# A pooling mixer in float32 by fast matrix products: all seven operands of a block kept in HBM between the two input phases

## The chip, the cores and the metric

One core of a Trainium2 chip. The metric is the time of one execution on the device, in microseconds; lower is better. TensorE (PE) multiplies, VectorE (DVE) adds and subtracts, ScalarE (ACT) copies and applies functions, GpSimd (POOL) and SyncE (SP) mostly issue DMAs. Every engine works through its own instructions in order.

## The reference

With `DEPTH = 1` one layer runs: a root-mean-square normalization, a causal pooling mixer, a residual addition and a last normalization, on `x` of 4096 rows by 1024 channels in float32.

```python
def pool_mixer(h, in_w, group_w, group_b, scale, out_w):
    b, s, _ = h.shape
    u, gate = jnp.split(h @ in_w, 2, axis=-1)
    ug = u.reshape(b, s, POOL_GROUPS, POOL_GROUP_DIM)
    pooled = jnp.stack([trailing_mean(ug[:, :, g], w) for g, w in enumerate(POOL_WINDOWS)],
                       axis=2) - ug
    mixed = jnp.einsum('bsgc,gcd->bsgd', pooled, group_w) + group_b
    y = mixed.reshape(b, s, POOL_WIDTH) * scale * jax.nn.silu(gate)
    return y @ out_w

h = h + pool_mixer(rms_norm(h, norm_w[0]), ...)
return rms_norm(h, final_norm_w)
```

## The kernel before, in words

**Products.** A float32 number is split into a high part (ScalarE copies it, which rounds it to fp32r) and a low part (VectorE subtracts the high one); a product takes three passes, high by high, high by low and low by high. Each large product is computed by seven products of half size, P1 to P7, instead of eight, with sums and differences of the quarters as operands (a Winograd form). `w[i]` holds the split weights of product i, `ops` is a ring of four buffers of split operands, two of which one product takes. PSUM has eight banks: P1, P2, P7 and P4 work in banks 0 to 3 ("x", "v"), P6, P5 and P3 in banks 4 to 7 ("y"). P1's result is copied to the y banks, on which P6, P5 and P3 add up; P4 adds to P7's.

**Phases.** The input weight is folded with the group map in the beginning. Then come 28 steps "a" (four blocks of 1024 rows by seven products, order P1, P2, P7, P6, P5, P4, P3) for one half of the output columns, 28 steps "b" for the other half with the same rows, and steps "o" for the output product, eight blocks of 512 rows by seven (order P1, P7, P6, P2, P5, P4, P3). A plain product of a or b has 48 matmuls of 512 columns: 2 halves of the contraction (h), 4 column tiles (ct), 2 tiles of 128 (kk), 3 passes.

**Operands of a and b.** `xs[b]` holds the quarters of a block's normalized rows: "11", "12" (second half of the rows), "21" and "22". In phase a `load_in` fetches them from `x`, `form_in` normalizes them by factors that were computed from `x` a block ahead and that take a way through HBM (`store_rs`, `load_rstd`, both on POOL's queue; `rd`), and forms the operands: "21" becomes 11 - 21 (P7), "2" = 22 - 21 (P6), "11" becomes 11 + "2" (P5), `form_s4` turns "12" into 12 - "2" (P3); P4 takes "22" itself. `split_in` splits an operand and, where `sd[b]` has an entry, stores it to HBM from POOL's queue (512 KB a half). Before the change that is so for P1, P2, P7 and P4. In phase b these four are loaded from `sd` on SP's queue, and "2", "11" and "12" are formed once more. `load` runs three steps ahead of the product, `form` two, `split_step` one.

**Inner P7.** For blocks 1 and 2 of phase b, P7 is itself made of seven products of half its size (`split_seven`, `product_seven`, 84 matmuls of 256 columns; P6's operand is split in its middle). The summed weights lie in three kept buffers (`kept_in`) and in a quarter of `w[P7][0]` that holds another weight in the plain form. `form_seven` prepares them in block 0 of phase b; `load_plain` and `split_plain` bring the plain quarter back in block 2, since block 3 uses the plain P7.

**Output weights.** `make_wo` scales and combines the output weights in blocks 1 and 2 of phase b and stores them to `wod`. In block 3, behind each product i, `load_w(wod, i)` loads that product's output weights (2 x 512 KB) and splits them into `w[i]`, which is free then.

**Output phase.** From block 2 on P7 is an inner product with own weights (`own_into`, prepared by `split_weight(P7, ...)` in steps of block 1), and P2 from block 1 on (`product_inner`, sets "spare" of banks). `add_inner(0, (0, 0))` adds an inner result from a spare bank to the rows; the inner P6 in step P5 writes that bank again. `norm_row` scales a finished row by its factor and sends it to the output. `steady` writes out the order of blocks 2 to 7; in the last block (`final`) the order by hand ends in step P2 (`InOrder.on`), and the scheduler places the rest.

**Order.** The scheduler orders the instructions of an engine by their place in the program and by when it expects their inputs; `tc.issue_after(ins)` puts what it covers behind `ins` on the same engine. `take` gives the buffer that was freed first, of 11 "st" and 8 "vt" (each 512 KB); who takes one that is still read waits.

Of the kernel before, what the change touches and what calls it, by code (L numbers as in the profile page):

```python
# [10 lines left out]
F32 = mybir.dt.float32  # L11
# [9 lines left out]
NB = S // TB  # L21
# [65 lines left out]
def kernel(  # L87
# [115 lines left out]
    def split(dst, src):  # L203
# [17 lines left out]
        for i in range(P1, P7 + 1)  # L221
# [3 lines left out]
            i: [dram.tile([P, 2, H], F32, name=f"sd{b}_{i}_{h}") for h in range(2)]  # L225
            for i in (P1, P2, P7, P4)
        }
# [346 lines left out]
    def load_saved(b, i):  # L574
# [17 lines left out]

    def form_in(q, b, i):

        s = xs[b]
        if i in (P1, P2):
            if q == 0:
                for u in s["11" if i == P1 else "12"]:
                    normalize(b, 0, u)
        elif i == P7:  # L600
            if q == 0:
                for h in range(2):
                    normalize(b, 1, s["21"][h])
                    sub(s["21"][h], s["11"][h], s["21"][h])
        elif i == P6:
            s["2"] = [take(pool=early if (q, b) == (0, 0) else None) for _ in range(2)]
            for h in range(2):
                if q == 0:
                    normalize(b, 1, s["22"][h])
                sub(s["2"][h], s["22"][h], s["21"][h])  # L610
            if not inner_in(q, b, P7):
                for u in s.pop("21"):
                    give(u)
            if q == 0:
                give(rstd.pop(b))
        elif i == P5:
            for h in range(2):
                add(s["11"][h], s["2"][h], s["11"][h])
            if (q, b) != (0, 0) and not inner_in(q, b, P7):
                for u in s.pop("2"):  # L620
                    give(u)

    def inner_in(q, b, i):

        return q == 1 and 0 < b < NB - 1 and i == P7

    def split_in(q, b, i):
        s = xs[b]
        if inner_in(q, b, i):
            return split_seven(s)  # L630
        key = {P1: "11", P2: "12", P6: "2", P7: "21", P5: "11", P4: "22", P3: "12"}[i]
# [62 lines left out]
    def form_seven(stage):  # L694
# [31 lines left out]
        if stage == 3:  # L726
            for u in seven.pop("raw"):
                give(u)

    def load_plain():  # L730
        seven["plain"] = take("p (n k c) -> p n k c", n=2, k=2)
        sync.dma_start(out=seven["plain"][:, 0], in_=t3d[0][:, :, 0:256])

    def split_plain():
        u = seven.pop("plain")
        home = [w[P7][0][:, v, :, 0:256] for v in range(2)]
        copy(home[0], u[:, 0])
        sub(home[1], u[:, 0], home[0].bitcast(F32))
        give(u)

# [626 lines left out]
    def evict_o(b, i, sets):  # L1367
# [4 lines left out]
        if inner and i == P2:  # L1372
            inner["rows"] = [hs[b][0, j][:, 0] for j in range(2)]
        elif inner and i == P5:
            product_inner(P5)
            add_inner(0, (0, 1), (1, 1))
            inner.clear()
            if final:
                for j in range(2):
                    early_half(0, j, 0)  # L1380
        for j in range(2):
# [24 lines left out]
            if last:  # L1406
                factors.append(late_factor(half, j, parts))
                if i == P4 and j == 1 or i == P3 and j == 0:
# [65 lines left out]
    def run(n, between=None, behind=None, seeds=4):  # L1474
# [4 lines left out]
        if kind == "o":  # L1479
            product_out(i, split_up.pop(n), sets, n == len(steps) - 1)  # L1480
            evict_o(b, i, sets)
        else:
            q = 0 if kind == "a" else 1
            if inner_in(q, b, i):
                us, parts = xs[b]["2"], []
                at["split"] += 1

                def next_half():
                    parts.append(split_half(us[len(parts)]))

                product_seven(split_up.pop(n), sets["v"], next_half, next_half)
                if b == NB - 2:
                    give_kept(*places_in)
                split_up[n + 1] = parts
            else:
                product_in(i, split_up.pop(n), sets, i == P1, between, behind)
            if "second" in seven:
                seven.pop("second")()
            evict_in(b, q, i, sets, seeds)
            if "third" in seven:  # L1500
                seven.pop("third")()
            if inner_in(q, b, i):
                form_s4(b)
                for u in xs[b].pop("2"):
                    give(u)
# [3 lines left out]
    def steady(n):  # L1509
# [87 lines left out]
        elif i == P2:  # L1597
# [4 lines left out]
            ready[P4] = next_op("p (s a b) -> p s a b", **whole)  # L1602
            split(ready[P4], s["22"])
            give(s.pop("22"))
            if final:
                norm_row(b - 1, 0, 1)
            InOrder.on = not final
            product_out(P2, ready.pop(P2), sets, False)
            evict_o(b, P2, sets)
        elif i == P5:  # L1610
            sub(s["12"], s["12"], s["11"])
# [6 lines left out]
        elif i == P4:  # L1618
            if not final:
                ahead["12"] = load_y(c, 0, 1)  # L1620
# [233 lines left out]
    def split_reach(kind, b, i):  # L1854
        if kind == "b" and 0 < b < NB - 1 and i == P6:
            return 0
        return 2 if kind == "o" and (b, i) != (0, P1) else 1

    def row_plan(b):
# [16 lines left out]
        (1, P6): lambda: sum_inner(P7),  # L1876
        (1, P5): lambda: split_weight(P7, P7, P6),
        (1, P4): lambda: (split_weight(P7, P5, P3), keep_temps(P7)),
    }
    forming_seven = (P7, P6, P5, P4)  # L1880

    for n in range(2, len(steps)):
# [72 lines left out]
        if kind in ("a", "b"):  # L1955
# [15 lines left out]
            if kind == "b" and b == NB - 1 and i == P3:  # L1971
# [57 lines left out]
```

## Time and profile before

| | |
|---|---|
| median of 3 runs | 906.92 us (906.7 to 907.47) |
| the profiled execution | 907.23 us, of which the span from the first to the last instruction is 905.4 |
| matmuls | 4518 |
| moved by DMA | 180.49 MB, mean 199 GB/s |
| granted TensorE clock | 0.998 of full speed |
| phase a, without what comes ahead of it | about 33 to 323 us |
| phase b | 323 to 613 us |
| phase o | 613 us to the end |

A row of the timeline begins with the start and the length in us, then the engine, the line (L79 is a helper through which all instructions but matmuls go, L807 the plain product, L753 the inner P7 of phase b, L949 the inner products of phase o), the operation, the tile written <- the tiles read, and the count; brackets hold the idle time before it and who ended it. A row of the chain of waits has the start, the length and what. Matmuls overlap, so that one with a length of 0.38 us can follow the one before after 0.22 us; TensorE's pace is found by dividing a stretch by its count.

### The profile page before, as it was taken

Reading aid. Unit: us, or ns where it says so; the run is one execution under the profiler, and the core shown is the slowest. Engines: PE = TensorE matmul, PEld = TensorE weight load, DVE = VectorE, ACT = ScalarE, POOL = GpSimd, SP = SyncE. Lnnn points to the kernel's source line nnn. Section 1 sums busy time; section 2 is a strip of 40 time slices with the busy share of each in tenths; the row PEclk is TensorE's granted clock in tenths of the full one; section 3 lists DMA queues with packets and bytes.
Section 4 is the critical chain, followed back from the end, with each engine's and each line's share of the span. In section 5 each row is a group of like instructions: output and inputs, shape, how many; then the busy total and the mean of one; then the engine's idle time right before and its main releaser. Section 6 shows DMA issues by size and latency. Waiting matters only on the chain.

```text
span 905.4 us, 12216 instructions
## 1 busy us (share of the span) xinstructions
PE 895.8 (99%) x4518; PEld 791.1 (87%) x4518; DVE 757.0 (84%) x925; ACT 517.5 (57%) x853; POOL 118.5 (13%) x208
## 2 busy tenths in 40 slices
PE   9999999999999999999999999999999999999996
PEld 7888888888888888889889888888889899999995
DVE  3899995985995999797599499599798878888797
ACT  7869547547445565346545636654657466565464
POOL 0020100100110000000000000001133333343330
PEclk9999999999999999999999999999999999999999
DMA  9987767577675453333554474638483865945953
GB/s 343 401 305 226 273 239 241 187 274 233 235 267 198 164 199 103 99 112 111 202 199 135 179 279 143 197 117 239 143 236 88 212 180 147 233 153 131 259 181 116
DMA packets 71692, 180.49 MB, mean 199 GB/s; under 512 B 6608, under 2 KB 24656, under 8 KB 71632
## 3 DMA queue, kind: packets, MB, share of 16 engines
q1 hardware_dynamic: 54976, 132.50, 42.6%
q0 software_dynamic: 15936, 46.16, 17.6%
q10 hardware_dynamic: 720, 1.06, 0.3%
q8 instruction: 35, 0.57, 0.3%
q14 instruction: 25, 0.20, 0.1%
HBM read 118.86 MB, written 60.83 MB: 198 GB/s over the span
## 4 chain that ended last, share of the span: by engine, by line
PE 87%; DVE 5%; ACT 3%; DMA 2%; issue 2%; POOL 0%; SPq 0%; DVEq 0%; ACTq 0%; POOLq 0%
PE bank L807 78%; PE bank L949 5%; DVE vt L79 2%; PE bank L753 2%; DVE op L79 2%; DMA st<-yd 1%; PE bank L447 1%; DVE st L79 1%; ACT op L79 1%; DMA early<-in_wut 1%; ACT st L79 1%; ACT w L79 0%; ACT vt L79 0%; DMA st<-wod 0%; DVE w L79 0%
## 5 line engine op out<-in xcount | busy, mean ns | idle before, releaser
L807 PE MATMUL bank<-op,w 128*128 128x512 f32 x2592 | 560.9, 379 | 0.1
L807 PEld LDWEIGHTS bank<-op,w 128*128 128x128 f32 x2592 | 489.4, 189 | 70.3 <-ACT vt L79 0.5
L807 PE MATMUL bank<-w,op 128*128 128x512 f32 (+1 forms) x1044 | 230.5, 377 | 0.0
L807 PEld LDWEIGHTS bank<-w,op 128*128 128x128 f32 x1044 | 192.3, 189 | 25.0
L79 DVE TENSOR_TENSOR op<-st,op 128x1024 fp32r<-128x1024 f32 x116 | 141.0, 1222 | 49.7 <-ACT op L79 49.3
L79 ACT ACTIVATE op<-st 128x1024 fp32r<-128x1024 f32 x116 | 121.4, 1051 | 68.7 <-PE bank L807 27.6
L79 ACT ACTIVATE op<-vt 128x1024 fp32r<-128x1024 f32 x67 | 70.4, 1053 | 59.3 <-DVE vt L79 38.7
L79 ACT ACTIVATE vt<-bank 128x512 f32<-128x512 f32 (+1 forms) x124 | 69.6, 580 | 48.0 <-PE bank L807 44.2
L79 DVE TENSOR_TENSOR op<-vt,op 128x1024 fp32r<-128x1024 f32 x67 | 80.9, 1221 | 17.5 <-ACT op L79 17.4
L79 DVE TENSOR_TENSOR st<-st,st 128x1024 f32<-128x1024 f32 (+1 forms) x55 | 63.9, 1181 | 17.6 <-ACT st L79 16.8
L79 POOL DMA_DIRECT2D vt<-in_x x26 | 23.3, 937 | 390.7 <-DVE vt L79 353.8
L79 ACT ACTIVATE bank<-bank 128x512 f32<-128x512 f32 (+1 forms) x78 | 38.7, 498 | 43.5 <-PE bank L807 32.1
L79 DVE TENSOR_TENSOR vt<-bank,vt 128x512 f32<-128x512 f32 (+1 forms) x94 | 54.2, 603 | 7.1 <-PE bank L949 4.6
L79 ACT ACTIVATE st<-bank 128x512 f32<-128x512 f32 (+1 forms) x58 | 33.0, 587 | 31.2 <-PE bank L807 17.4
L79 ACT ACTIVATE st<-st 128x1024 f32<-128x1024 f32 x33 | 34.8, 1056 | 22.6 <-DVE st L79 19.6
L79 DVE TENSOR_TENSOR st<-bank,st 128x512 f32<-128x512 f32 (+1 forms) x68 | 41.2, 625 | 7.4 <-PE bank L807 4.1
L79 DVE TENSOR_TENSOR st<-st,vt 128x1024 f32<-128x1024 f32 (+1 forms) x36 | 41.6, 1175 | 2.2 <-DMA vt<-rd 2.2
L949 PEld LDWEIGHTS bank<-w,op 128*128 128x128 f32 x312 | 40.4, 191 | 1.7
L949 PE MATMUL bank<-w,op 128*128 128x256 f32 x312 | 41.1, 275 | 0.0
L79 DVE TENSOR_TENSOR w<-st,w 128x1024 fp32r<-128x1024 f32 (+1 forms) x27 | 31.6, 1182 | 9.3 <-ACT w L79 9.2
L79 DVE TENSOR_TENSOR_SCAN vt<-vt,window 128x1040 f32<-128x1040 f32 x16 | 38.0, 2381 | 0.3 <-DMA yd<-vt 0.3
L79 DVE TENSOR_TENSOR vt<-vt 128x1024 f32<-128x1024 f32 (+3 forms) x42 | 37.6, 898 | 0.1
(115 smaller groups left out, 720.7 us busy)
## 6 DMA issues: line engine op xcount, KB each, us to landing
st<-in_xt SPq DMA_DIRECT2D x28, 512.0 KB, 6.2
sd<-st POOLq DMA_DIRECT2D x28, 512.0 KB, 4.4
st<-sd SPq DMA_DIRECT2D x26, 512.0 KB, 4.5
st<-in_x SPq DMA_DIRECT2D x21, 512.0 KB, 6.3
yd<-st SPq DMA_DIRECT2D x19, 512.0 KB, 2.9
vt<-yd SPq DMA_DIRECT2D x17, 512.0 KB, 10.4
out<-vt POOLq DMA_DIRECT2D x17, 512.0 KB, 3.3
st<-wod SPq DMA_DIRECT2D x16, 512.0 KB, 4.3
```

The costliest lines, as they stand in the source:

```text
L79: r = f(*args, **kwargs)
L447: latest[0] = nc.tensor.matmul(ps, a[:, kk, 2 * j + t, :], maps, start=t + m == 0, stop=t == 1 and m == len(pairs) - 1,).ins
L753: latest[0] = nc.tensor.matmul(cell(n, c).rearrange("p (a s) -> p a s", s=2), x1, x2, start=i == P1 and k + m == 0, stop=k == 1 and m == 2 ...
L807: latest[0] = nc.tensor.matmul(ps, a, b, start=start and n == 0, stop=stop and n == 2, skip_group_check=True).ins
L949: latest[0] = nc.tensor.matmul(ps, x1, x2, start=start and k + n == 0, stop=k == 1 and n == 2, skip_group_check=True,).ins
```

## The change

In phase a all seven operands of a block are stored to `sd` (P6's, P5's and P3's are new), and in phase b each of the seven is loaded three steps ahead of its product and its buffers are given back once it is split, so that phase b forms nothing. Block 3 of phase b computes P7 by the inner form too: the kept buffers are held one block longer, and `load_plain` and `split_plain` are gone. In block 3 the output weights of P1 are loaded and split behind P7, those of P2 and P7 behind P6, those of P6 and P5 behind P5, those of P4 and P3 behind their own products as before. In block 1 of phase o the four splits of `split_weight(P7, ...)` all stand in step P4, where two were in step P5. In the last block of phase o the first inner result is added ahead of P2's two evictions, P4's operand is split behind them, and the scaling of one row of the block before (`norm_row(b - 1, 0, 1)`) moves from step P2 to step P4.

```diff
--- before
+++ after
@@ -223,7 +223,7 @@
     sd = [
         {
             i: [dram.tile([P, 2, H], F32, name=f"sd{b}_{i}_{h}") for h in range(2)]
-            for i in (P1, P2, P7, P4)
+            for i in range(P1, P7 + 1)
         }
         for b in range(NB)
     ]
@@ -579,63 +579,59 @@
+    operand = {P1: "11", P2: "12", P7: "21", P6: "2", P5: "11", P4: "22", P3: "12"}
+
     def load_in(q, b, i):
         s = xs[b]
-        if i == P1:
-            s["11"] = load_saved(b, P1) if q else load_x(b, 0, 0)
-        elif i == P2:
-            s["12"] = load_saved(b, P2) if q else load_x(b, 0, 1)
-        elif i == P7:
-            s["21"] = load_saved(b, P7) if q else load_x(b, 1, 0)
-        elif i == P6:
-            s["22"] = load_saved(b, P4) if q else load_x(b, 1, 1)
-
-    def form_in(q, b, i):
+        if q:
+            s[operand[i]] = load_saved(b, i)
+        elif i in (P1, P2, P7, P6):
+            key, *place = {
+                P1: ("11", 0, 0), P2: ("12", 0, 1), P7: ("21", 1, 0), P6: ("22", 1, 1)
+            }[i]
+            s[key] = load_x(b, *place)
+
+    def form_in(b, i):
...
         elif i == P6:
-            s["2"] = [take(pool=early if (q, b) == (0, 0) else None) for _ in range(2)]
+            s["2"] = [take(pool=early if b == 0 else None) for _ in range(2)]
             for h in range(2):
-                if q == 0:
-                    normalize(b, 1, s["22"][h])
+                normalize(b, 1, s["22"][h])
                 sub(s["2"][h], s["22"][h], s["21"][h])
...
     def inner_in(q, b, i):
 
-        return q == 1 and 0 < b < NB - 1 and i == P7
+        return q == 1 and b > 0 and i == P7
 
     def split_in(q, b, i):
...
-        if i == P6 and (q or b):
+        if i == P6 and q == 0 and b:
             form_s4(b)
-        if i not in (P1, P2, P7, P6):
+        if q or i not in (P1, P2, P7, P6):
             for u in s.pop(key):
                 give(u)
         return t
@@ -726,17 +722,6 @@
-    def load_plain():
-        seven["plain"] = take("p (n k c) -> p n k c", n=2, k=2)
-        sync.dma_start(out=seven["plain"][:, 0], in_=t3d[0][:, :, 0:256])
-
-    def split_plain():
-        u = seven.pop("plain")
-        home = [w[P7][0][:, v, :, 0:256] for v in range(2)]
-        copy(home[0], u[:, 0])
-        sub(home[1], u[:, 0], home[0].bitcast(F32))
-        give(u)
@@ -1371,6 +1356,8 @@
         if inner and i == P2:
             inner["rows"] = [hs[b][0, j][:, 0] for j in range(2)]
+            if final:
+                add_inner(0, (0, 0))
...
-        if inner and i == P2:
+        if inner and i == P2 and not final:
             add_inner(0, (0, 0))
@@ -1453,8 +1440,8 @@
     def form(n):
         kind, b, i = step(n)
-        if kind in ("a", "b"):
-            form_in(kind == "b", b, i)
+        if kind == "a":
+            form_in(b, i)
@@ -1489,7 +1476,7 @@
-                if b == NB - 2:
+                if b == NB - 1:
                     give_kept(*places_in)
...
             if inner_in(q, b, i):
-                form_s4(b)
                 for u in xs[b].pop("2"):
                     give(u)
@@ -1600,13 +1586,15 @@
             ready[P4] = next_op("p (s a b) -> p s a b", **whole)
-            split(ready[P4], s["22"])
-            give(s.pop("22"))
-            if final:
-                norm_row(b - 1, 0, 1)
+            if not final:
+                split(ready[P4], s["22"])
+                give(s.pop("22"))
             InOrder.on = not final
             product_out(P2, ready.pop(P2), sets, False)
             evict_o(b, P2, sets)
+            if final:
+                split(ready[P4], s["22"])
+                give(s.pop("22"))
...
         elif i == P4:
-            if not final:
+            if final:
+                norm_row(b - 1, 0, 1)
+            else:
                 ahead["12"] = load_y(c, 0, 1)
@@ -1852,7 +1842,7 @@
     def split_reach(kind, b, i):
-        if kind == "b" and 0 < b < NB - 1 and i == P6:
+        if kind == "b" and b > 0 and i == P6:
             return 0
@@ -1874,8 +1864,7 @@
-        (1, P5): lambda: split_weight(P7, P7, P6),
-        (1, P4): lambda: (split_weight(P7, P5, P3), keep_temps(P7)),
+        (1, P4): lambda: (split_weight(P7, P7, P6, P5, P3), keep_temps(P7)),
@@ -1957,17 +1946,13 @@
             if kind == "b" and b == NB - 1:
-                load_w(wod, i)
+                for p in {P1: (), P2: (), P7: (P1,), P6: (P2, P7), P5: (P6, P5)}.get(i, (i,)):
+                    load_w(wod, p)
             if kind == "b" and b in (1, 2) and i == P7:
                 load_wo(b - 1)
-                if b == NB - 2:
-                    load_plain()
...
-            if kind == "b" and b == NB - 2 and i == P4:
-                with tc.issue_after(latest_copy[0]), tc.issue_after(latest_split[0]):
-                    split_plain()
```

More of the change, by code (lines that the diff above doesn't have):

```diff
@@ L580, in load_saved @@
         return us
+    operand = {P1: "11", P2: "12", P7: "21", P6: "2", P5: "11", P4: "22", P3: "12"}
     def load_in(q, b, i):
         s = xs[b]
-        if i == P1:
-            s["11"] = load_saved(b, P1) if q else load_x(b, 0, 0)
-        elif i == P2:
-            s["12"] = load_saved(b, P2) if q else load_x(b, 0, 1)
-        elif i == P7:
-            s["21"] = load_saved(b, P7) if q else load_x(b, 1, 0)
-        elif i == P6:
-            s["22"] = load_saved(b, P4) if q else load_x(b, 1, 1)
-    def form_in(q, b, i):
+        if q:
[6 more added lines that the diff above has]
+    def form_in(b, i):
         s = xs[b]
         if i in (P1, P2):
-            if q == 0:
-                for u in s["11" if i == P1 else "12"]:
-                    normalize(b, 0, u)
+            for u in s["11" if i == P1 else "12"]:
+                normalize(b, 0, u)
         elif i == P7:
[L601 to L604, printed above, removed]
+            for h in range(2):
+                normalize(b, 1, s["21"][h])
+                sub(s["21"][h], s["11"][h], s["21"][h])
         elif i == P6:
-            s["2"] = [take(pool=early if (q, b) == (0, 0) else None) for _ in range(2)]
+            s["2"] = [take(pool=early if b == 0 else None) for _ in range(2)]
             for h in range(2):
-                if q == 0:
-                    normalize(b, 1, s["22"][h])
+                normalize(b, 1, s["22"][h])
                 sub(s["2"][h], s["22"][h], s["21"][h])
-            if not inner_in(q, b, P7):
-                for u in s.pop("21"):
-                    give(u)
-            if q == 0:
-                give(rstd.pop(b))
+            for u in s.pop("21"):
+                give(u)
+            give(rstd.pop(b))
         elif i == P5:
@@ L618, in form_in @@
                 add(s["11"][h], s["2"][h], s["11"][h])
-            if (q, b) != (0, 0) and not inner_in(q, b, P7):
+            if b:
                 for u in s.pop("2"):
@@ L630, in split_in @@
             return split_seven(s)
-        key = {P1: "11", P2: "12", P6: "2", P7: "21", P5: "11", P4: "22", P3: "12"}[i]
+        key = operand[i]
         later = q == 0 and b == 0 and i in (P1, P2)
@@ L728, in form_seven @@
                 give(u)
-    def load_plain():
-        seven["plain"] = take("p (n k c) -> p n k c", n=2, k=2)
-        sync.dma_start(out=seven["plain"][:, 0], in_=t3d[0][:, :, 0:256])
-    def split_plain():
-        u = seven.pop("plain")
-        home = [w[P7][0][:, v, :, 0:256] for v in range(2)]
-        copy(home[0], u[:, 0])
-        sub(home[1], u[:, 0], home[0].bitcast(F32))
-        give(u)
     def product_seven(t, v, middle, end):
```

## The prediction

> **What bounds the kernel now.** I read the engines' shares first, then TensorE's instructions in order of time, where brackets hold the idle time before one and what ended it.
>
> ```profile
> span 905.4 us, 12216 instructions
> ...
> PE 895.8 (99%) x4518; PEld 791.1 (87%) x4518; DVE 757.0 (84%) x925; ACT 517.5 (57%) x853; POOL 118.5 (13%) x208
> ```
> ```profile
> 46.55 370.93 PE L807 MATMUL bank<-op,w 128*128 128x512 f32 x1716
> ...
> 498.68 114.46 PE L807 MATMUL bank<-op,w 128*128 128x512 f32 x528
> ...
> 671.19 0.94 PE L949 MATMUL bank<-inner,op 128*128 128x256 f32 x6 [0.31 <-DVE vt L79]
> ...
> 885.05 0.94 PE L949 MATMUL bank<-inner,op 128*128 128x256 f32 x6 [0.61 <-DVE vt L79]
> ```
>
> TensorE is busy for 99% of the span, and over 895 us it stands still for VectorE only twice, 0.31 us at 671 and 0.61 us at 885. A busy TensorE need not be a fast one, so I divide: 370.93 us for 1716 matmuls is 0.216 us each, and 114.46 for 528 is 0.217. The pace is the same early and late, so there is no hidden gap to win back in the two input phases. Time can fall only by fewer matmuls, by those two waits, or by the tail; it can rise by any new wait.
>
> **The inner P7 of the last block.** The chain of waits gives both forms of a product:
>
> ```profile
> 417.48 9.60 PE bank L753 x84
> 427.08 62.16 PE bank L807 x288
> 489.24 9.60 PE bank L753 x84
> ```
>
> The 288 matmuls are six plain products of 48, so one costs 62.16 / 6 = 10.36 us. The inner form in blocks 1 and 2 takes 9.60 us both times. The third one saves 0.76 us. Its additions (four half-size subtractions, two operand halves more to split, eight quarter-size moves on ScalarE) lay beside the products in blocks 1 and 2, where TensorE waited for nothing. Without that cover, the two splits alone are 2 x 1.22 us of VectorE.
>
> [...]
>
> **The subtractions and loads of the second phase.** Removed are 2 for P6, 2 for P5, 2 for P3 in each of four blocks, 24 in all. The second view is that of the stages: a block each, with its length, the busy time of TensorE's matmuls, its weight loads, VectorE, ScalarE and POOL, the granted clock, the DMA engines' share and GB/s.
>
> ```profile
> L79 DVE TENSOR_TENSOR st<-st,st 128x1024 f32<-128x1024 f32 (+1 forms) x55 | 63.9, 1181 | 17.6 <-ACT st L79 16.8
> ```
> ```profile
> 33.00:105.60 72.60, 72.60 (x341) 63.42 (x340) 64.87 (x84) 55.98 (x86) 11.07 (x21) 1.00 0.79 290
> 105.60:178.20 72.60, 72.60 (x338) 63.58 (x337) 62.45 (x75) 40.27 (x66) 6.49 (x12) 1.00 0.67 225
> ...
> 323.40:396.00 72.60, 72.60 (x338) 63.56 (x338) 64.00 (x76) 36.50 (x52) 0.00 (x0) 1.00 0.41 137
> ...
> 541.20:613.80 72.60, 72.54 (x336) 63.22 (x335) 62.64 (x60) 41.64 (x57) 0.00 (x0) 1.00 0.46 156
> ```
>
> At 1.18 us each this is 7 us of VectorE per block, 28 in all, but it lies under a TensorE that is busy 72.60 of 72.60 us. I cost it at nothing; it is slack, not time.
>
> In its place come 24 stores on POOL's queue in the first phase and 24 loads on SP's queue in the second, 512 KB (0.524 MB) each.
>
> ```profile
> q1 hardware_dynamic: 54976, 132.50, 42.6%
> q0 software_dynamic: 15936, 46.16, 17.6%
> ```
>
> By their shares, POOL's queue used 0.176 x 905.4 / 46.16 = 3.45 us of the 16 DMA engines per MB and SP's 2.91, so 1.81 us per store and 1.53 per load. Six stores add 10.9 us to a block of 72.6 (0.15 of the engines), six loads 9.2 (0.13). The loads raise the share from 0.41 to about 0.54 in the second phase: harmless, as each load is issued three products (31 us) ahead of its use, and the four operands loaded earlier now leave their buffers earlier. The stores raise block 0 from 0.79 to 0.94, and there the stages matter:
>
> ```profile
> 57.00:67.50 10.50, 10.50 (x50) 9.21 (x49) 10.50 (x11) 6.57 (x9) 1.60 (x3) 1.00 1.02 368
> 67.50:78.00 10.50, 10.50 (x50) 9.19 (x50) 10.50 (x14) 10.47 (x18) 0.00 (x0) 1.00 0.64 235
> 78.00:88.00 10.00, 10.00 (x48) 8.77 (x47) 8.50 (x14) 10.00 (x15) 1.10 (x2) 1.00 0.70 175
> 88.00:98.50 10.50, 10.50 (x50) 9.19 (x50) 8.34 (x16) 5.03 (x10) 1.50 (x3) 1.00 1.00 401
> ```
> ```profile
> 93.83 1.23 DVE L79 TENSOR_TENSOR st<-st,vt 128x1024 f32<-128x1024 f32 x1 [2.16 <-DMA vt<-rd]
> ...
> 101.06 1.22 DVE L79 TENSOR_TENSOR op<-st,op 128x1024 fp32r<-128x1024 f32 x1
> ```
>
> From 67.5 to 88 the DMA engines are idle for 3.8 + 3.0 = 6.8 us, so some 4 of the 10.9 us reach the next stage, which is full. There VectorE already waits 2.16 us for the broadcast row factors of block 1 (vt<-rd), and behind that wait stand the normalization and the operand of block 1's P1. That operand's second half is ready at 102.3. Block 1 starts at 46.55 + 276 x 0.216 = 106.2 (36 matmuls of P2 and five products) and needs that half 1.3 us later: 5.2 us of cover against 4. I take nothing here; the bounds are nothing and 10.9 - 5.2 = 5.7 us, if all six stores went ahead of the factors.
>
> POOL's own queue has room:
>
> ```profile
> L79 POOL DMA_DIRECT2D sd<-st x28: 531/535/546, 52.3 to 268.5; - x28
> ```
>
> Six more issues of 0.535 us per block are 3.2 us beside 6 to 11 us busy; what queues behind a store there is the store and load of the row factors. The buffers of P6, P5 and P3 are complete before they are split, so their stores can land before the split frees them.
>
> [...]
>
> **Output weights split behind the block.** Before, one pair of weights was loaded and split behind each product; P1's and P2's pairs now wait until P7 and P6, P6's until P5.
>
> ```profile
> 559.47 1.06 ACT L79 ACTIVATE w<-st 128x1024 fp32r<-128x1024 f32 x1 [5.88 <-DMA st<-wod]
> 560.44 1.07 ACT L79 ACTIVATE vt<-bank 128x512 f32<-128x512 f32 x2
> ```
>
> ScalarE stood 5.88 us before such a load, and P2's evictions behind it came so late that P7 lost 0.06 us (72.54 in the window above). That place is now free of weights: 0.06 gained. The price moves: behind P6 and behind P5 stand four loads and four splits, 4 x 1.22 = 4.9 us of VectorE in one piece. Operands are split ahead:
>
> ```profile
> 596.23 1.22 DVE L79 TENSOR_TENSOR op<-st,op 128x1024 fp32r<-128x1024 f32 x1
> ```
>
> This is P3's second half, ready at 597.5 and needed at 498.68 + 114.30 - 24 x 0.216 = 607.8: 10 us of cover. I take nothing. The removed reload of the quarter of P7's weights (two half-size splits, one DMA) and the inner-weight splits moved one step later lie under the same cover.
>
> **The last block of the output phase.** The wait at 885 ends with the third addition of this row:
>
> ```profile
> 881.04 1.22 DVE L79 TENSOR_TENSOR op<-vt,op 128x1024 fp32r<-128x1024 f32 x1
> 882.18 1.28 DVE L79 SCALAR_TENSOR_TENSOR vt<-vt,ors,st 128x1024 f32<-128x1024 f32 x1
> 883.37 1.62 DVE L79 TENSOR_TENSOR vt<-bank,vt 128x512 f32<-128x512 f32 x3
> ...
> 895.20 0.41 DVE L79 SCALAR_TENSOR_TENSOR columns<-columns 128x1 f32<-128x1 f32 x2
> 895.76 0.69 DVE L79 TENSOR_TENSOR vt<-bank,vt 128x512 f32<-128x512 f32 x1
> ```
>
> The addition that frees the bank goes first, and the low half of P4's operand (1.22) and the scaling of a row (1.28) behind it; the bank is free by 881.5, so the 0.61 us go. But the moved work does not vanish: VectorE runs without a gap into the tail, and at 895.61 it is only 0.15 us ahead of the bank of P3 that TensorE ends at 895.74. If TensorE comes 0.61 earlier, VectorE decides. Bounds: a gain of 0.61, and a loss of 0.67 where all 1.28 us of scaling fall behind the last eviction that TensorE waits to end. I take half of the wait, 0.3. The wait at 671 has VectorE's chain in front of it and stays.
>
> **Sum.** 0.76 + 0.06 + 0.3 = 1.1 us off. The profiled execution took 907.23 us (span 905.4 and 1.8 around it): 906.1. The median of the runs, 906.92, is 0.3 below it, so the forecast is 905.8.
>
> **Rivals.** *Weights in the way (slower).* ScalarE's wait of 5.88 us recurs behind P7, where P6's evictions are next. P6's first bank is complete 6.5 us into its product and P5 writes it at 10.4, so 3.9 less the 0.6 of an eviction is covered and 2.6 us are paid: 908.4. If the groups of four wait twice, 11.8 us, their 10 us of cover fails too: 1.8 more, 910.2. For it: it just failed to cost in the profile. Against it: fewer operands hold buffers, and P2's step is free.
>
> *Stores before the row factors (slower).* It decides from 5.2 us of delay on, up to 905.8 + 5.7 = 911.5. For it: stages at 1.00 of the DMA engines. Against it: the stores come early, and block 1 has a share of only 0.67. [...]
>
> *Only the matmuls.* VectorE's tail eats the 0.3, and 906.2 is left, or 907.0 with the loss above.
>
> *All waits go.* 0.76 + 0.06 + 0.31 + 0.61 = 1.74: 905.2 from the median, and below 905.1 with any help in the tail.
>
> **Chances.** Forecast 42%, only the matmuls 15%, weights in the way 20% (half at 908.4, half at 910.2 and over), stores 11%, all waits 12%. A measurement of this kernel tells about 0.2% from no change, 1.8 us: 905.1 to 908.7. Inside are the forecast, "only the matmuls" and the mild half of the weights: 67%. Faster is the 12% of all waits; slower 10 + 11 = 21%. The range goes from 904.8 to 909.8, which leaves out part of the two slow cases. The likeliest case alone has 905.2 to 906.4.
>
> **What would show it.** 84 matmuls at L753 a third time, near 560, in 9.6 us; a DMA share near 0.9 in block 0 with TensorE still at 72.60; no VectorE subtraction on loaded operands in the second phase; no wait at 885. A wait of TensorE between 570 and 613, or near 106, would prove the forecast wrong, and so would a span that falls by more than 1.8 us.

## The result and the profile after

The change makes the kernel slower: 915.77 us (median of 6 runs) against 907.14 for the kernel before on the same chip (6 runs), a ratio of 1.0096 with a 95% interval of 1.0076 to 1.0117. The forecast was 905.8 us and its range 904.8 to 909.8. The profiled execution took 915.82 us. Its page of the profile has these lines:

```profile
span 914.0 us, 12390 instructions
...
PE 897.3 (98%) x4554; PEld 792.4 (87%) x4554; DVE 735.4 (80%) x908; ACT 521.2 (57%) x862; POOL 130.4 (14%) x232
...
DMA packets 78332, 205.40 MB, mean 225 GB/s; under 512 B 7360, under 2 KB 25152, under 8 KB 78272
```

VectorE has 21.6 us less to do, as intended, and 25 MB more are moved. TensorE's instructions in order of time show where the time went; the inner P7 is L738 now, the plain product L792.

```profile
45.97 28.92 PE L792 MATMUL bank<-op,w 128*128 128x512 f32 x132
75.69 1.56 PE L792 MATMUL bank<-op,w 128*128 128x512 f32 x6 [0.80 <-ACT st L79]
77.78 144.01 PE L792 MATMUL bank<-op,w 128*128 128x512 f32 x666 [0.53 <-ACT st L79]
225.98 198.56 PE L792 MATMUL bank<-op,w 128*128 128x512 f32 x912 [4.19 <-ACT st L79]
424.38 2.84 PE L738 MATMUL bank<-op,w 128*128 128x256 f32 x24
...
563.35 6.74 PE L792 MATMUL bank<-op,w 128*128 128x512 f32 x30 [0.87 <-ACT bank L79]
...
573.24 0.94 PE L738 MATMUL bank<-op,inner 128*128 128x256 f32 x6 [0.47 <-ACT st L79]
...
621.73 51.96 PE L792 MATMUL bank<-w,op 128*128 128x512 f32 x240
```

I take the starts of these rows and 0.2161 us for a matmul of 512 columns (370.77 us for 1716 in the kernel before). What a stretch takes beyond its count is lost time:

| place | worked out as | us |
|---|---|---|
| beginning | 45.97 - 46.55 | -0.58 |
| block 0 of phase a | 77.78 - 45.97 - 138 matmuls (29.82) | +1.99 |
| block 2 of phase a, the standstill before 225.98 | 225.98 - 77.78 - 666 matmuls (143.90) | +4.30 |
| behind that standstill | 424.38 - 225.98 - 912 matmuls (197.05) | +1.35 |
| from the first inner P7 to the output phase | 621.73 - 424.38, less 195.66 before | +1.69 |
| output phase to the end of the span | 914.0 - 621.73, less 292.42 before | -0.15 |
| sum | the spans: 914.0 - 905.4 | +8.60 |

**Block 0 and block 2.** The chain of waits (start, length, what) names both places:

```profile
60.41 9.42 DMA wvd<-early
...
75.15 0.48 ACT st L79
...
203.81 10.47 DMA st<-wvd
...
214.37 1.24 DVE st L79
215.63 3.49 DMA t3d<-st
...
219.18 4.82 DMA st<-wvd
224.02 1.24 DVE st L79
...
225.33 0.61 ACT st L79
```

At 60 us a store of the folded input weights (`wvd`) takes 9.42 us to land. The buffer that it reads holds P5's weights, whose split on ScalarE waits 1.93 us for it, and behind that split stand P6's evictions (the moves of P6's results out of the banks). At 204 us the weights are loaded back to form `t3` (`save_t3`: two loads, a subtraction, a store, two times over). The second load takes 10.47 us, and P6's evictions on ScalarE wait for the last of these subtractions, 7.63 us here and 3.29 before (first after, then before):

```profile
225.33 2.07 ACT L79 ACTIVATE st<-bank 128x512 f32<-128x512 f32 x4 [7.63 <-DVE st L79]
```
```profile
219.72 2.07 ACT L79 ACTIVATE st<-bank 128x512 f32<-128x512 f32 x4 [3.29 <-DVE st L79]
```

Both times TensorE waits for a bank that ScalarE has not yet emptied.

POOL's queue shows why the weight store of block 0 is late (in brackets the idle time before an issue):

```profile
57.96 0.53 POOL L79 DMA_DIRECT2D sd<-early  x1 [3.58 <-DVE early L79]
59.22 0.54 POOL L79 DMA_DIRECT2D sd<-early  x1 [0.73 <-DVE early L79]
59.81 1.13 POOL L79 DMA_DIRECT2D wvd<-early  x2
```

The first two rows are the new stores of P6. They have to wait for VectorE, and the last two weight stores wait behind them. For block 2 the DMA view of 190 to 226 us (issue, count, size, median us to landing) tells the rest, first after, then before:

```profile
sd<-st POOLq DMA_DIRECT2D x6, 512.0 KB, 7.7
st<-wvd SPq DMA_DIRECT2D x4, 512.0 KB, 7.6
...
sd<-vt POOLq DMA_DIRECT2D x2, 512.0 KB, 8.1
```
```profile
st<-wvd SPq DMA_DIRECT2D x4, 512.0 KB, 4.0
sd<-st POOLq DMA_DIRECT2D x2, 512.0 KB, 4.2
```

The loads of `t3` now run beside eight stores of operands instead of two, and their median is nearly twice as long. One of them sets the delay: the second load of the first pair took 10.47 us where it took 4.4 before. What follows it in the chain landed about as before: the store took 3.49 us (4.3 before), the last load 4.82 (4.7). So the first subtraction comes some 6 us late, and the rest of the chain is late by that one delay.

**Behind the standstill.** Windows of 2 us (busy time of TensorE, its weight loads, VectorE, ScalarE and POOL; then the granted clock, the DMA share, GB/s):

```profile
224.00:226.00 2.00, 0.02 (x1) 0.02 (x1) 1.23 (x1) 0.67 (x2) 0.56 (x1) 0.89 0.84 326
226.00:228.00 2.00, 2.00 (x5) 1.64 (x6) 0.00 (x0) 2.00 (x4) 0.00 (x0) 0.50 0.78 219
228.00:230.00 2.00, 2.00 (x9) 1.68 (x8) 0.00 (x0) 2.00 (x5) 0.00 (x0) 0.76 0.66 207
230.00:232.00 2.00, 2.00 (x11) 1.76 (x10) 1.23 (x1) 1.44 (x3) 0.00 (x0) 1.00 0.84 268
```

When TensorE resumes, its granted clock is 0.50 and then 0.76, and 5 and 9 matmuls fall into windows that hold 11 at full clock. 2.00 x 0.50 + 2.00 x 0.24 = 1.5 us of work are lost, close to the 1.35 of the table.

### The profile page after: what moved, and what is told of

Its sections match the earlier page's. It is cut to its first block, busy times and chain, and to the rows that moved or that the text cites. A ratio compares the mean times of both kernels' runs of the same rounds, so it can differ in the third digit from the quotient of the medians.

```text
span 914.0 us, 12390 instructions
## 1 busy us (share of the span) xinstructions
PE 897.3 (98%) x4554; PEld 792.4 (87%) x4554; DVE 735.4 (80%) x908; ACT 521.2 (57%) x862; POOL 130.4 (14%) x232
## 3 DMA queue, kind: packets, MB, share of 16 engines
q10 hardware_dynamic: 720, 1.06, 0.3%
## 4 chain that ended last, share of the span: by engine, by line
PE 70%; DVE 13%; DMA 7%; ACT 5%; issue 4%; POOL 1%; DVEq 0%; POOLq 0%; ACTq 0%; SPq 0%
PE bank L792 62%; DVE vt L79 6%; PE bank L934 4%; DVE st L79 4%; PE bank L738 3%; DVE op L79 3%; ACT st L79 2%; DMA st<-wvd 2%; DMA vt<-yd 1%; DMA wod<-vt 1%; DMA wvd<-early 1%; PE bank L447 1%; DMA st<-in_x 1%; ACT op L79 1%; ACT early L79 1%
## 5 line engine op out<-in xcount | busy, mean ns | idle before, releaser
L792 PE MATMUL bank<-op,w 128*128 128x512 f32 x2544 | 553.8, 380 | 6.6 <-ACT st L79 5.5
L792 PEld LDWEIGHTS bank<-op,w 128*128 128x128 f32 x2544 | 480.9, 189 | 77.6 <-ACT st L79 6.7
L792 PE MATMUL bank<-w,op 128*128 128x512 f32 (+1 forms) x1044 | 230.5, 377 | 0.0
L792 PEld LDWEIGHTS bank<-w,op 128*128 128x128 f32 x1044 | 192.3, 189 | 25.0
L79 DVE TENSOR_TENSOR op<-st,op 128x1024 fp32r<-128x1024 f32 x118 | 143.4, 1220 | 63.2 <-ACT op L79 62.9
L79 ACT ACTIVATE op<-st 128x1024 fp32r<-128x1024 f32 x118 | 123.6, 1052 | 65.6 <-PE bank L792 22.7
L79 DVE TENSOR_TENSOR st<-st,st 128x1024 f32<-128x1024 f32 (+1 forms) x49 | 53.7, 1109 | 25.9 <-ACT st L79 16.8
L79 POOL DMA_DIRECT2D st<-in_x x18 | 16.6, 960 | 366.2 <-ACT st L79 350.8
L79 ACT ACTIVATE bank<-bank 128x512 f32<-128x512 f32 (+1 forms) x84 | 40.9, 489 | 45.5 <-PE bank L792 32.6
L79 ACT ACTIVATE st<-bank 128x512 f32<-128x512 f32 (+1 forms) x62 | 35.1, 587 | 38.3 <-PE bank L792 20.1
L79 POOL DMA_DIRECT2D sd<-st x45 | 24.1, 535 | 129.4 <-DVE st L79 73.8
L79 DVE TENSOR_TENSOR st<-st,vt 128x1024 f32<-128x1024 f32 (+1 forms) x32 | 36.7, 1166 | 3.1 <-DMA vt<-rd 2.9
## 6 DMA issues: line engine op xcount, KB each, us to landing
vt<-yd SPq DMA_DIRECT2D x17, 512.0 KB, 10.9
```

The source lines that it names most:

```text
L79: r = f(*args, **kwargs)
L792: latest[0] = nc.tensor.matmul(ps, a, b, start=start and n == 0, stop=stop and n == 2, skip_group_check=True).ins
```

## Experiments

My theory after this reading: the stores cost the time, at two places of the first phase. The rival: the second phase (its loads, the inner P7, the output weights) costs it. Three stretches of each profiled execution tell them apart: "first", from TensorE's 46 us to the first inner P7; "second", from there to the output phase; "output", from there to the end of the span. Ratios are against the kernel before, timed beside (907.59, 907.29, 907.37 and 907.35 us in the four groups of rows). The stretches come from one profiled execution each, which is not the median one: those of fab, fa and f5 took 911.14, 915.51 and 910.91 us, 1.2 to 1.6 above their medians, and that of e5 took 905.61, 0.7 below.

| run | median us | ratio (95%) | first | second | output |
|---|---|---|---|---|---|
| before (profile above) | 907.14 | 1 | 370.77 | 195.66 | 292.42 |
| after | 915.77 | 1.0096 (1.0076 to 1.0117) | 378.41 | 197.35 | 292.27 |
| e1 stores only | 915.27 | 1.0092 (1.0077 to 1.0107) | 378.65 | 195.56 | 293.27 |
| e2 four stored | 907.99 | 1.0013 (1.0004 to 1.0022) | 370.64 | 195.02 | 294.07 |
| e3 last block | 907.45 | 1.0003 (0.9994 to 1.0013) | 370.64 | 195.48 | 293.17 |
| fab two moves | 909.57 | 1.0024 (1.0014 to 1.0035) | 372.00 | 197.75 | 293.46 |
| fa P6's stores moved | 914.26 | 1.0075 (1.0059 to 1.0090) | 377.11 | 196.96 | 293.39 |
| fb t3 moved | 911.04 | 1.0040 (1.0026 to 1.0054) | 372.91 | 197.25 | 292.60 |
| e4 stores, both moved | 908.28 | 1.0007 (0.9998 to 1.0016) | 371.66 | 195.44 | 292.97 |
| e5 four stored, early load | 906.35 | 0.9990 (0.9981 to 0.9999) | 370.65 | 195.28 | 291.80 |
| f5 three moves | 909.72 | 1.0028 (1.0017 to 1.0038) | 372.02 | 198.81 | 292.35 |
| f8 weight store first | 907.45 | 0.9999 (0.9990 to 1.0008) | 372.01 | 195.34 | 292.33 |

### e1: the stores alone

To the kernel before:

```diff
-            for i in (P1, P2, P7, P4)
+            for i in range(P1, P7 + 1)
```

Expected: 

> The kernel before with one thing added: the first phase also stores P6, P5 and P3 of every block (six stores of 512 KB more per block), and nothing loads them. Stores theory: the delays of block 0 (about 2.0 us: stores of P6 ahead of the last two weight stores) and of the place in block 2 where t3 is formed (about 4.3 us of standing still and 1.4 us of lowered clock behind it) come with the stores alone; so TensorE shows a wait of 4 us or so near 225 us with the granted clock below 0.8 behind it, and the time is 907.1 + 7.7 = 914.8 (913.5 to 916). Rival, costs of the second phase (its loads, the inner P7, the weights behind a product): no wait near 225 beyond what the kernel before has, and 907 to 908.

Measured: 915.27 us, 7.7 over the kernel before. One line brings back nearly the whole loss, at the same places:

```profile
76.59 1.56 PE L807 MATMUL bank<-op,w 128*128 128x512 f32 x6 [1.24 <-ACT st L79]
78.68 144.01 PE L807 MATMUL bank<-op,w 128*128 128x512 f32 x666 [0.53 <-ACT st L79]
226.59 198.64 PE L807 MATMUL bank<-op,w 128*128 128x512 f32 x912 [3.90 <-ACT st L79]
```

The second phase is as long as before (195.56). The rival falls for the bulk of the loss.

### e2: everything but the stores

To the kernel after: `sd` has four operands again, `load_in` and `form_in` are those of before, and the inner P7 of block 3, the schedule of the output weights and the last block stay as changed.

```diff
-            for i in range(P1, P7 + 1)
+            for i in (P1, P2, P7, P4)
...
-        if q:
-            s[operand[i]] = load_saved(b, i)
-        elif i in (P1, P2, P7, P6):
...
+        elif i == P6:
+            s["22"] = load_saved(b, P4) if q else load_x(b, 1, 1)
```

Expected: 

> The kernel after, but with four operands stored as before and P6, P5, P3 formed again in the second phase; all its other edits stay (inner P7 in the last block, the output weights split behind a product, the last block's order). Stores theory: no wait near 225 us, no lowered clock, and what is left are the second phase's edits: between 906.0 (as predicted without the stores) and 908.5 (if the inner P7 of the last block and the weights lose about 1.4 us, as in the trace of after). Rival, costs of the second phase: 912 or more.

Measured: 907.99. The first stretch is back at 370.64, and the second is 195.02, 0.64 shorter than before: the third inner P7 pays. But the output stretch is 1.65 longer. The first of these rows is VectorE's, the second TensorE's, at the wait that had 0.31 us before:

```profile
644.40 0.69 DVE L79 TENSOR_TENSOR st<-st,st 128x512 f32<-128x512 f32 x1 [1.36 <-DMA st<-wod]
```
```profile
671.46 0.94 PE L949 MATMUL bank<-inner,op 128*128 128x256 f32 x6 [1.62 <-DVE vt L79]
```

A load for the inner weights of P2 was issued at 639.76, where the kernel before issued its last one at 633.84, and VectorE's chain to 671 starts that much later.

### e3: the last block alone

To the kernel before, the last block of the output phase as in the change:

```diff
+            if final:
+                add_inner(0, (0, 0))
...
-        if inner and i == P2:
+        if inner and i == P2 and not final:
             add_inner(0, (0, 0))
...
         elif i == P4:
+            if final:
+                norm_row(b - 1, 0, 1)
```

Expected: 

> The kernel before with only the edits of the output phase's last block: addition that frees the bank first, low half of P4's operand behind the scaling steps, row scaling moved into P4. Predicted term: 0.3 us off (907.1 to 906.8), bounds 0.61 off and 0.67 on. Theory from the trace of after: TensorE's wait of 0.61 us at 885 is gone, but the work behind the last matmul grows from 7.0 to about 7.7 us, so the net is 0.1 to 0.2 us off. Rival: the longer tail comes from elsewhere in the change, and here the full 0.6 us is gained (906.5).

Measured: 907.45, no difference that can be told. TensorE's wait at 885 is gone, and its last group starts at 886.90 where it was 887.78 before; VectorE's last instruction, first here and then before, is not earlier:

```profile
886.90 10.61 PE L807 MATMUL bank<-w,op 128*128 128x512 f32 x60
```
```profile
901.14 0.88 DVE L79 SCALAR_TENSOR_TENSOR vt<-vt,columns,st 128x256 f32<-128x256 f32 x2
```
```profile
900.73 0.88 DVE L79 SCALAR_TENSOR_TENSOR vt<-vt,columns,st 128x256 f32<-128x256 f32 x2
```

VectorE sets the end; what TensorE gains waits in the tail. From the start of TensorE's last group to the start of VectorE's last instruction it is 14.24 us instead of 12.95: 1.29 more, the 1.28 of the moved scaling.

### fab, fa, fb: moving the two places

To the kernel after; fa has the first of these edits, fb the second, fab both. What is `later` is stored behind the weights.

```diff
-        later = q == 0 and b == 0 and i in (P1, P2)
+        later = q == 0 and b == 0 and i in (P1, P2, P6)
...
-        if kind == "a" and b == 2 and i == P7:
+        if kind == "a" and b == 2 and i == P4:
             save_t3()
```

Expected: 

> The kernel after with two moves in the first phase and nothing left out: in block 0 the stores of P6 go behind the last weight stores in the queue, and t3 is formed and stored in block 2's P4 in place of P7, away from the stores of P6. Stores theory: both delays of the first phase go, 915.8 - 2.0 - 5.7 = 908.1 (907 to 909.5). Rival (the transfers are too many for the first phase wherever they stand): the waits come back elsewhere in block 1 or 2 and the time stays above 912.

> The kernel after with one move: in block 0 the stores of P6 go behind the last two weight stores in POOL's queue. Stores theory, by place: the wait for the weight store goes (1.9 us of ScalarE), but in the trace with both moves an eviction of P6 then waited 1.40 us for a buffer whose store had not landed, and TensorE lost 0.82 us there in place of 2.0; so 1.2 off and the 4.2 us wait near 225 untouched: 914.5. Rival (the two delays are one, the first pushes the second): the wait near 225 shrinks too, and the time falls below 912.

> The kernel after with the other move: t3 is formed and stored in block 2's P4 in place of P7. Stores theory: the wait near 225 and the lowered clock behind it go, 4.2 + 1.4 = 5.6 off, less up to 1 us that then shows in the last block and at the start of the output phase, where VectorE and ScalarE are late whatever TensorE does: 910.2 to 911.2, with the 2.0 us of block 0 still there. Rival: the transfers delay another place of block 2 or 3, and the time stays above 913.

Measured: 909.57 with both, 914.26 and 911.04 with one each. The wait at 225 and the low clock are gone wherever t3 is moved, so that place is worth 5.5 us of the first stretch (378.41 to 372.91). The first delay is worth 1.3 alone (378.41 to 377.11): less than the 1.99 us lost there, because with the weight stores in time another wait shows. ScalarE, with both moves:

```profile
67.18 2.02 ACT L79 ACTIVATE w<-early 128x1024 fp32r<-128x1024 f32 x2
...
74.76 0.60 ACT L79 ACTIVATE st<-bank 128x512 f32<-128x512 f32 x1 [1.40 <-DMA sd<-st]
```

The split of the weights no longer waits, but the first eviction of P6 wants a buffer whose store has not landed. fa and fb came out as expected; fab is 1.5 us above the 908.1 named for it, just over its upper bound, and its second stretch (197.75 against 195.66 before) says that most of this is not the first phase's. What fb does not separate: at the new place the four loads of `t3` take 5.6 us in the median instead of 7.6, and P6's evictions no longer wait for its subtractions at all. Which of the two removed the wait stays open.

### e4: what 24 stores cost when they delay neither place

The kernel of e1 with the two moves of fab:

```diff
-            for i in (P1, P2, P7, P4)
+            for i in range(P1, P7 + 1)
...
+        later = q == 0 and b == 0 and i in (P1, P2, P6)
...
+        if kind == "a" and b == 2 and i == P4:
```

Expected: 

> The kernel before with the six extra stores per block (not loaded) and both moves. Stores theory by place: the transfers cost only what block 0 still pays for buffers held by their stores, 0.8 us: 907.6 + 0.8 = 908.4 (907.8 to 909), and TensorE has no wait near 225. Rival (the second phase pays for what is left with both moves in the kernel after, 2 us): about 907.6 here. Second rival (12.6 MB more of traffic cost by themselves): 909.5 or more.

Measured: 908.28, TensorE without a wait near 225. So 12.6 MB more of stores cost about 1 us at these places, where an eviction of P6 still waits 1.06 us for a buffer that is being stored, and most of the remaining loss of fab (909.57) belongs to its second phase.

### e5: the late load of e2

To e2:

```diff
-        (0, P4): lambda: load_inner(P2),
+        (0, P5): lambda: load_inner(P2),
```

Expected: 

> The kernel after with four operands stored (as in the second experiment) and one move: the two loads from which the output phase's inner weights of P2 are formed are issued one product earlier in its first block. In the second experiment VectorE waited 1.36 us for the second of them at 643 and TensorE 1.62 us at 671. Late-load theory: TensorE's wait there falls back to 0.3 us, 908.0 - 1.3 = 906.7, about 0.1% under the kernel before; the inner P7 of the last block then pays its 0.76. Rival (VectorE has too much to do before 671, and the product gained is waited for whatever the load does): the wait stays at 1.0 us or more, and the time at 907.5 to 908.

Measured: 906.35, 0.1% faster than the kernel before, the only one of these kernels that is. TensorE's wait is 0.32 us:

```profile
670.22 0.94 PE L949 MATMUL bank<-inner,op 128*128 128x256 f32 x6 [0.32 <-DVE vt L79]
```

### f5 and f8: the second phase with seven loads

f5 is fab with the edit of e5 (`(0, P5): lambda: load_inner(P2)`). Expected: 

> The kernel after, all seven operands stored and loaded, with the three moves: P6's stores of block 0 behind the weight stores, t3 in block 2's P4, and the output phase's two loads for the inner weights of P2 one product earlier. Place theory (the second phase's loads cost nothing by themselves; what the kernel with two moves still lost against the stores alone, 909.6 - 908.3 = 1.3, is the wait of 1.58 us at 675 for that late load): 908.3 (907.7 to 909). Rival (seven loads and the scans beside P1 of the last block set the end): 909.2 or more, with waits of TensorE of 1 us or more between 550 and 560 that the output phase does not take back.

Measured: 909.72. The theory fell: the wait at 675 did go (0.31), but the time did not, and in the profiled execution the second stretch is 198.81. VectorE, ScalarE and TensorE of f5:

```profile
528.50 4.66 DVE L79 TENSOR_TENSOR_SCAN vt<-vt,window 128x1040 f32<-128x1040 f32 x2 [2.15 <-DMA wod<-vt]
```
```profile
554.15 0.23 ACT L79 ACTIVATE vt<-tails 128x32 f32<-128x32 f32 x1 [5.45 <-DMA yd<-vt]
554.29 1.06 ACT L79 ACTIVATE bank<-bank 128x512 f32<-128x512 f32 x2
```
```profile
554.92 2.86 PE L792 MATMUL bank<-op,w 128*128 128x512 f32 x12 [1.82 <-ACT bank L79]
558.37 6.74 PE L792 MATMUL bank<-op,w 128*128 128x512 f32 x30 [0.59 <-ACT bank L79]
```

These rows suggest a chain: an output weight is formed in a "vt" buffer and stored (`wod<-vt`); a scan of the pooling waits 2.15 us for that buffer; the scans and what follows them run late; ScalarE waits 5.45 us for one of their buffers and only behind that wait copies P1's banks; TensorE waits 1.82 and 0.59 us for the copies. How long the store takes to land sets the wait. From the DMA view of 520 to 530 us, in f5 and then in e5:

```profile
wod<-vt SPq DMA_DIRECT2D x1, 512.0 KB, 6.1
```
```profile
wod<-vt SPq DMA_DIRECT2D x1, 512.0 KB, 4.2
```

Landings of 4.2 (e5), 5.1 (fb), 5.5 (fab) and 6.1 us (f5) go with waits of the scan of 0.25, 1.11, 1.52 and 2.15 us, and with waits of TensorE at that place of nothing, 0.53, 1.17 and 1.82. In after and fa the store lands in 4.6 and 4.3 us and the scan waits 0.69 and 0.31; there TensorE waits at the next copies only, 0.87 and 0.68 us. Taken together, its waits at both copies are 0.68 (fa), 0.87 (after), 1.37 (fb), 1.78 (fab) and 2.41 us (f5): in each case the scan's wait and 0.2 to 0.4 more. In the kernels before and e4 this weight lies in an "st" buffer at that place, and no scan waits. In f8 that weight, P5's, is formed and stored first of its group, in `combine`:

```diff
+        t1 = take()
+        sub(t1, b12, b11)
         sub(b12, b22, b12)
         add(b11, b12, b11)
         sub(b21, b21, b11)
-        t1 = take()
-        sub(t1, b22, b11)
-        return {P6: b11, P7: b12, P5: t1, P4: b21, P3: b22}
+        return {P5: t1, P6: b11, P7: b12, P4: b21, P3: b22}
```

Expected: 

> The kernel of the run with all three moves, and P5's output weight (the difference of the two blocks it is algebraically equal to, so it needs no earlier sum) formed and stored first of its group in place of last. In that run a scan of VectorE in block 2 waited 2.15 us for the buffer that this store holds, and TensorE 1.82 us for bank copies of the last block's P1 at 555; over five runs the second was the first less 0.3 to 0.6. Chain theory: the store lands some 10 us earlier, the scan does not wait, the 1.8 us at 555 go and at least part of the 0.6 at 558: 909.7 - 1.8 to 2.4 = 907.3 to 907.9, which is the stores alone (908.3) less the inner P7's 0.76. Rival (ScalarE's wait for the store of the pooled rows, 5.4 us, sets that place whatever the scan does): the wait at 555 stays above 1 us and the time above 909.

Measured: 907.45, level with the kernel before. The store is issued at 516.10 instead of 522.32 (6 us earlier, not 10), the scan does not wait, and both waits in block 3's P1 are gone; one before the inner P7's second group stays. VectorE and TensorE of f8:

```profile
524.98 4.65 DVE L79 TENSOR_TENSOR_SCAN vt<-vt,window 128x1040 f32<-128x1040 f32 x2
```
```profile
499.60 62.33 PE L792 MATMUL bank<-op,w 128*128 128x512 f32 x288
...
565.08 0.94 PE L738 MATMUL bank<-op,inner 128*128 128x256 f32 x6 [0.48 <-ACT st L79]
```

The second stretch falls from 198.81 to 195.34, 3.5 us, between two profiled executions; the medians are 2.3 us apart. With its first link taken away the chain is gone. But the edit does a second thing: the first subtraction of the group now reads two other blocks and starts at 514.45 instead of 515.92. The scan comes 3.52 us earlier, and only 2.15 of that are the wait for the store. So the chain has the series of runs and this edit for it; what the store's place alone is worth was not separated.

## Why the prediction was wrong

**The step that failed** is the price of the new stores, the passage that ends "I take nothing here; the bounds are nothing and 10.9 - 5.2 = 5.7 us". They cost 7.7 us alone (e1), more than its upper bound, and 915.77 lies above the worst time that a rival named (911.5). The mean shares that it worked out were nearly right: the DMA share of block 0 (33 to 105.6 us) became 0.88 where it worked out 0.94. But TensorE was busy for 71.27 of these 72.60 us: the waits are not in the means. Three parts of the step were wrong.

- It looked for the price at one place, the row factors of block 1. VectorE waited 2.90 us for them instead of 2.16, and TensorE not at all. The words "what queues behind a store there is the store and load of the row factors" leave out the last two weight stores of block 0, which the new stores of P6 were put ahead of, on the same queue: 1.3 us (fa).
- That "their stores can land before the split frees them" does not hold in block 0: with both moves (fab) an eviction waits 1.40 us for a buffer that is still being stored.
- It read the DMA share of block 0 by stages, that of block 1 as a mean, and block 2 not at all. Block 2 has a chain of loads and stores, t3, for whose end P6's evictions wait. One load of it that took 10.47 us instead of 4.4 made the chain some 6 us late, and 4.30 of that reached TensorE. Moving t3 by three products wins 5.5 us with the same traffic, so the place sets the price, not the amount moved.

Then came a cost that no step had: the lowered clock behind the standstill, 1.35 us.

A smaller slip: over the span TensorE stood still for VectorE three times, not two; the third wait (0.21 us at 23 us) lies ahead of the phases and changes no term.

**The loads and subtractions of the second phase** at nothing: the removed subtractions are worth nothing, as predicted, but the stretch is not free of loss. "Fewer operands hold buffers" missed which buffer the next taker gets: with the edits of e2 already, P5's output weight holds a "vt" buffer until its store lands, and with seven operands loaded that store takes 0.1 to 1.9 us longer to land than in e5. The edit of f8 took 198.81 - 195.34 = 3.5 us from the profiled stretch and 2.3 us from the median. In the change itself the stretch is 1.69 longer in all, though the inner P7 takes 0.76 off: the waits seen are 0.87 at 563 and 0.47 at 573, and the way from the first inner P7 to the second is 0.55 longer (72.31 against 71.76 us); some 0.6 were not taken apart. Why the store takes longer was not isolated either: from 520 to 530 us f5 moves less than e5 (297 against 361 GB/s).

**Inner P7, 0.76:** right in its direction, and not all of it arrives: the stretch is 0.64 shorter than before in e2, 0.38 in e5 and 0.32 in f8; in the change itself the waits of block 3 swallow it. **Output weights:** ScalarE's wait of 5.88 us did not come back (its longest for such a load is 1.67) and the rival "weights in the way" did not come true at its place; what remains is P1's weight split ahead of the first moves of the inner P7, 0.47 us. **The last block, 0.3:** the wait at 885 went and the moved work took the gain back, as the step's own doubt said; no gain can be told (e3).

Without stores the sum, 1.1 us off, nearly came true as a number: e5, which is the change without the new stores and loads and with one late load mended, is 0.9 us faster than the kernel before. Its terms did not come true one by one, so part of that is luck: in the profiled execution 0.48 us lie ahead of phase a, where no edit acts, the second stretch gives 0.38 of the 0.82 named for it, and the output phase gives 0.62, where the last block alone (e3) gave nothing. The outcome of the change hung on what was put at zero.

## What to carry to other kernels

An added transfer is priced by who stands behind it (the same 24 stores cost 7.7 us in e1 and about 1 us at the places of e4): list for each queue what follows the new issue, and for each chain load - compute - store - load who waits for its end and how much later it may come, before looking at mean bandwidth. A removed computation that was hidden buys nothing (the second stretch is 195.34 us in f8, which has none of the 24 subtractions, and 195.28 in e5, which has them all), while the buffers that replace it are taken from someone; ask which buffer the next taker gets and what its release waits for. A wait taken away on one engine shows the next one (in fab ScalarE's 1.93 us for a weight store went, and 1.40 us for the store of an operand came), so a gain of half a microsecond should be followed to the end of the span.

## What the runs showed of the hardware

The granted TensorE clock fell to about half after standstills of 4.19 us (after: 0.50 and 0.76 from 226 to 230 us), 3.90 (e1: 0.58 and 0.57 from 226 to 230) and 3.09 (fa), and not after one of 1.62 us (e2). In fa, after 3.09 us:

```profile
224.00:226.00 2.00, 1.28 (x6) 1.15 (x7) 0.00 (x0) 1.93 (x5) 0.00 (x0) 0.98 0.55 152
226.00:228.00 2.00, 2.00 (x7) 1.53 (x6) 0.00 (x0) 2.00 (x5) 0.00 (x0) 0.50 0.69 266
228.00:230.00 2.00, 2.00 (x8) 1.64 (x7) 0.83 (x1) 2.00 (x5) 0.00 (x0) 0.66 0.77 227
```

And in e2, around its wait of 1.62 us:

```profile
669.00:671.00 2.00, 0.83 (x4) 0.38 (x2) 2.00 (x3) 1.49 (x3) 0.00 (x0) 1.00 1.07 221
671.00:673.00 2.00, 1.54 (x10) 1.47 (x11) 2.00 (x5) 0.00 (x0) 0.00 (x0) 1.00 1.08 241
```

The low clock comes when TensorE has resumed or is about to (in after it resumes at 225.98 us, and the window from 224 to 226 has 0.89 already). I estimate that it lasts about 3 us: the 1.5 us of work lost in the windows from 226 to 230 us are 3 us at half the clock. So the place with the standstill of 4.19 us costs 4.30 + 1.35 = 5.65 us in all. What it is in a standstill that lowers the clock, these runs do not tell.

Open: the first phase of fab, f5 and f8 is still 1.2 us longer than before; part of it is the eviction that waits for a stored buffer, and the rest was not taken apart.
